# adaLN columns by transposes, and a routing whose shift stands inside the product sets

## The chip, the cores and the metric

One core of a Trainium2 chip runs the whole program. The metric is the device time of one execution in microseconds (us). TensorE multiplies, VectorE and ScalarE work elementwise, GpSimd does a few small powers, and the queue of SyncE (SP) issues the weight transfers. A single engine's instructions run in the order written into its queue.

## The reference

Two layers over 256 rows of 1024 features: a gated linear attention, then a gated recurrence, each followed by 16 experts of which two work on a row. All arithmetic is in 32-bit floats. In each layer six vectors of 1024 come from the conditioning vector (shift, scale and gate, for the mixer and for the experts): this is called adaLN here.

```python
def rmsnorm(x, g):
    inv = lax.rsqrt(jnp.mean(x * x, axis=-1, keepdims=True) + EPS)
    return (x * inv) * g

def modulate(h, shift, scale):
    return h * (1 + scale[:, None]) + shift[:, None]

def gla_mixer(h, w_in, w_gate_up, b_gate, norm_g, w_out):
    proj = h @ w_in
    q, k, v, g, a_lr = jnp.split(proj, [512, 1024, 2048, 3072], axis=-1)
    log_a = jax.nn.log_sigmoid(a_lr @ w_gate_up + b_gate) / 16
    # chunks of 64 rows: cumulative sums of log_a, decayed k, a state per chunk
    # S_n = diag(G_n) S_{n-1} + k_dec^T v,  o = q S_n,  o = rmsnorm(o) * silu(g)
    return o @ w_out

def lru_mixer(h, w_in, ...):
    gate_br, xb = jnp.split(h @ w_in, 2, axis=-1)
    # causal convolution of 4 taps, two gates by 4 blocks of 256, a scan over time
    return (hs * jax.nn.gelu(gate_br)) @ w_out

def grouped_moe(h, router_w, router_bias, w_gate, w_up, w_down):
    scores = jax.nn.sigmoid(h @ router_w)
    # the group with the best two biased scores, the best two experts in it
    for e in range(16):
        he = jax.nn.silu(h @ w_gate[e]) * (h @ w_up[e])
        out = out + combine[:, e:e + 1] * (he @ w_down[e])
    return out

def reference(x, c, ...):
    cond = jax.nn.silu(c)
    for i in range(2):
        sh1, sc1, g1, sh2, sc2, g2 = jnp.split(cond @ ada_w[i] + ada_b[i], 6, axis=-1)
        h = modulate(rmsnorm(x, norm_mix_g[i]), sh1, sc1)
        mix = gla_mixer(h, ...) if i == 0 else lru_mixer(h, ...)
        x = x + g1[:, None] * mix
        h = modulate(rmsnorm(x, norm_ffn_g[i]), sh2, sc2)
        x = x + g2[:, None] * grouped_moe(h, router_w, ...)
    return rmsnorm(x, final_norm_g)
```

## The kernel before, in words

**Weights.** Nearly all bytes are weights, 285 MB, and each is used once. They stream through a ring of 17 slots of 1 MB (`Stream`, `SLOTS`). `plan` writes the order out by hand; `stream.get` takes the next slot and lets the queue run ahead. The queue issues in that order, and a transfer whose slot is still in use holds all behind it. The same ring also lends slots to large intermediate tiles (`big`).

**adaLN.** Each of the six vectors per layer needs a product of 1024 by 1024, read as two halves of 512 columns, 2 MB each. `fill` does a half on VectorE: eight multiply-adds (L335, L333) leave 128 partial sums per column in `acc`, at a lower priority than the rest. `fill_now` does it on TensorE in four quadrants (L354) and copies the result (L356), which leaves each column's four sums in rows 0, 32, 64 and 96. What is left is put in `owed`, and `settle` finishes it: for a gate vector, wanted along the free dimension, a product with ones (L365) and a copy; for shifts and scales, wanted as one column of a partition each, a product with ones or with the selector `quad` (L368), a masked product with the identity (L370), a reduction (L371), and small sums with the tables (L373 to L376). `bent` applies a scale and a shift to a transposed tile of features (L438 on ScalarE, L440 on VectorE).

**First layer.** `gla` normalizes x, transposes it (L448) and needs the mixer's columns in two halves. `bend(0)` computes the first column set, settles it and bends four of the eight feature tiles; then three token projections take their first halves (L565), `bend(1)` does the second set, the low-rank products follow (L575), and then the second halves, with the gate's cumulative sums (L595, L598) between the second and the third projection.

**Out product and routing.** `out_route` multiplies by the out weights in four parts (L488), adds to x (L490, L491) and routes in between, with TensorE's order fixed as written. Behind the third settle stand `router` (the router's weights times the scale, L803; the shift's share of the scores, a tiny product, L806, spread over the rows, L808), then the parts of the second row block, with transposes and `logits` (L817) between products. `choose` picks experts on VectorE, `route_count` counts rows (L855, L858), `gather_tile` collects rows (L908), and `route_order` sorts the experts by load. Only then are the routed weights' addresses known (L937), and their transfers can be issued (L263).

**Experts.** `moe` runs seven units: the first with two experts that are always loaded, the others in the order found. A unit is two up products (L1016), an activation (L1133, L1134), transposes (L1145), a down product (L1027) and a scatter into x (L1046, L1047). Unit 0 also spreads the row weights and settles what is owed; units 3 and 4 transpose h for `overflow`, a branch for rows that found no room, which the data of this run doesn't enter. The last unit runs in column parts (L1038).

## Time and profile before

| | |
|---|---|
| time, median of 3 runs | 796.24 us (795.29 to 800.42) |
| profiled execution, its own time | 796.28 us |
| its span | 794.5 us |
| TensorE busy (its share) | 729.8 us (92%) |
| VectorE busy | 356.0 us (45%) |
| ScalarE busy | 137.5 us (17%) |
| HBM read | 284.54 MB, 359 GB/s over the span |

Busy shares are means over stages with different limits, and TensorE's ends are modelled, so 92% doesn't say that TensorE sets the time. The rows below are read by stage: who waits, for whom, and whether the DMA engines are full at that time. PE is TensorE (PEld its weight loads), DVE VectorE, ACT ScalarE, POOL GpSimd, SPq the queue of SyncE.

### The profile page before, as it was taken

What the parts mean: (1) busy time and instruction counts of PE and PEld (TensorE: products, weight loads), DVE (VectorE), ACT (ScalarE), POOL (GpSimd) and SP (SyncE); (2) the same over time, 40 slices, a digit from 0 to 9 for tenths busy, and PEclk for the clock granted to TensorE, in tenths of its full rate; (3) what the DMA queues carried; (4) which work ended last, traced back from release to release, by engine and by line L of the source; (5) the groups of instructions that cost most, each with busy time, mean ns of one, the idle gap of its engine ahead of it and who ended that gap; (6) DMA issues with size and microseconds to landing.
All of it is one profiled execution on the core that took longest, in us unless ns stands there. A gap on an engine that the chain in (4) does not pass through costs nothing. (4 is left out here: it accounts for less than half of the span.)

```text
span 794.5 us, 9656 instructions
## 1 busy us (share of the span) xinstructions
PE 729.8 (92%) x3591; PEld 357.0 (45%) x3591; DVE 356.0 (45%) x809; ACT 137.5 (17%) x271; POOL 27.1 (3%) x69
## 2 busy tenths in 40 slices
PE   4889999988999999998978999978899999999984
PEld 3333664445353353353215888635553353353322
DVE  3225876687462142231114389985632233222114
ACT  4104213021120011010003147121120011010002
POOL 4000001000000000000000005000000000000000
PEclk9899999999999999999998999989799999999999
DMA  9999969678879999999999999982599999999994
GB/s 297 386 387 387 385 239 318 202 282 361 342 317 423 419 421 422 420 419 413 420 370 378 375 363 332 403 326 106 230 408 397 420 420 419 421 422 407 421 379 156
DMA packets 80445, 286.27 MB, mean 360 GB/s; under 512 B 5991, under 2 KB 16280, under 8 KB 57866
## 3 DMA queue, kind: packets, MB, share of 16 engines
q1 hardware_dynamic: 78752, 284.71, 92.2%
q10 hardware_dynamic: 1258, 0.66, 0.3%
q8 instruction: 30, 0.49, 0.3%
q0 software_dynamic: 384, 0.23, 0.1%
q14 instruction: 21, 0.17, 0.1%
HBM read 284.54 MB, written 1.05 MB: 359 GB/s over the span
## 5 line engine op out<-in xcount | busy, mean ns | idle before, releaser
L1016 PE MATMUL ps<-w 128*32 128x512 f32 (+1 forms) x1280 | 201.8, 594 | 4.8 <-DMA w<-in_moe_w_up_dram 2.9
L1016 PEld LDWEIGHTS ps<-w 128*32 128x32 f32 (+1 forms) x1280 | 62.5, 121 | 137.7 <-issue 120.2
L1027 PE MATMUL ps<-w,s 128*32 128x512 f32 (+1 forms) x512 | 85.0, 594 | 2.8 <-ACT s L1147 2.8
L1047 DVE TENSOR_TENSOR x<-x,ps 128x512 f32<-128x512 f32 (+1 forms) x60 | 39.1, 652 | 56.7 <-PE ps L1046 56.6
L488 PE MATMUL ps<-w 128*128 128x512 f32 x128 | 61.6, 627 | 0.0
L1046 PE MATMUL ps<-mid,s 128*128 128x512 f32 (+1 forms) x120 | 55.1, 581 | 2.9 <-DVE mid L1155 2.6
L1134 DVE TENSOR_TENSOR s<-s,ps 128x512 f32<-128x512 f32 x14 | 9.6, 686 | 105.6 <-PE ps L1016 105.6
L733 PE MATMUL ps<-hT,w 128*128 128x256 f32 x256 | 56.7, 384 | 0.0
L333 DVE SCALAR_TENSOR_TENSOR acc<-w,cond,acc 128x512 f32<-128x512 f32 x70 | 54.0, 801 | 0.7
L733 PEld LDWEIGHTS ps<-hT,w 128*128 128x128 f32 x256 | 49.4, 194 | 6.9
L1027 PEld LDWEIGHTS ps<-w,s 128*32 128x32 f32 (+1 forms) x512 | 25.6, 123 | 58.3 <-issue 51.8
L565 PE MATMUL ps<-w,hT 128*128 128x512 f32 x96 | 46.3, 638 | 3.5 <-issue 3.5
L1166 DVE TENSOR_TENSOR mid<-ps,gate 128x512 f32<-128x512 f32 x24 | 16.6, 692 | 63.2 <-PE ps L1027 63.2
L890 PE MATMUL ps<-onehot,h 128*128 128x256 f32 x192 | 42.4, 379 | 0.0
L333 DVE SCALAR_TENSOR_TENSOR gate<-w,cond,gate 128x512 f32<-128x512 f32 x56 | 40.9, 747 | 0.9
L890 PEld LDWEIGHTS ps<-onehot,h 128*128 128x128 f32 x192 | 36.5, 190 | 7.5 <-issue 2.4
L1133 ACT ACTIVATE s<-ps 128x512 f32<-128x512 f32 x14 | 8.4, 599 | 164.4 <-PE ps L1016 164.4
L488 PEld LDWEIGHTS ps<-w 128*128 128x128 f32 x128 | 24.4, 201 | 25.5 <-issue 24.0
L1046 PEld LDWEIGHTS ps<-mid,s 128*128 128x128 f32 x120 | 20.5, 190 | 30.8 <-issue 20.8
L565 PEld LDWEIGHTS ps<-w,hT 128*128 128x128 f32 x96 | 19.2, 204 | 28.4 <-issue 27.9
L1147 ACT COPY s<-ps 128x512 f32<-128x512 f32 x14 | 8.2, 586 | 136.1 <-PE ps L1145 136.1
L370 DVE TENSOR_TENSOR s<-ps,ident 128x512 f32<-128x512 f32 x16 | 10.6, 680 | 43.3 <-PE ps L368 43.3
(267 smaller groups left out, 688.8 us busy)
## 6 DMA issues: line engine op xcount, KB each, us to landing
w<-in_moe_w_gate_dram SPq DMA_DIRECT2D x64, 1024.0 KB, 10.0
w<-in_moe_w_up_dram SPq DMA_DIRECT2D x64, 1024.0 KB, 13.1
w<-in_moe_w_down_dram SPq DMA_DIRECT2D x56, 1024.0 KB, 15.8
w<-in_ada_w_dram SPq DMA_DIRECT2D x48, 1024.0 KB, 11.6
w<-in_gla_w_in_dram SPq DMA_DIRECT2D x12, 1024.0 KB, 14.5
w<-in_moe_w_down_dram SPq DMA_DIRECT2D x16, 512.0 KB, 10.0
w<-in_lru_w_in_dram SPq DMA_DIRECT2D x8, 1024.0 KB, 12.4
w<-in_gla_w_out_dram SPq DMA_DIRECT2D x4, 1024.0 KB, 4.8
```

Source lines behind the costliest of these rows:

```text
L333: V.scalar_tensor_tensor(acc, w, cond[:, k:k + 1], acc, op0=OP.mult, op1=OP.add)
L370: V.tensor_tensor(own, ps.rearrange("p (q j) -> p q j", j=4), ident[:, :, None].to_broadcast([P, P, 4]), op=OP.mult)
L488: T.matmul(ps, yT[:, k, m * P:(m + 1) * P], w[k // 2][:, k % 2, sl], start=k == 0, stop=k == 7)
L565: T.matmul(pst[i][m], hT[:, 4 * b + j, m * P:(m + 1) * P], w[:, j], start=b == 0 and j == 0, stop=b == 1 and j == 3)
L733: T.matmul(ps[:, 0:S], w[k // 4][:, k % 4, ct * P:(ct + 1) * P], hT[:, k, :], start=k == 0, stop=k == 7)
L890: T.matmul(ps[j // 2][:, j % 2 * 2 * P:(j % 2 + 1) * 2 * P], hv[:, b, j, :], oh, start=m == 0 and j % 2 == 0, stop=m == 1 and j % 2 == 1, ...
L1016: T.matmul(ps[p0:p0 + n], xg[:, k, t0 + p0:t0 + p0 + n], w[i][:, j, :], start=k == 0, stop=k == 7)
L1027: T.matmul(ps[hf][p0:p0 + n], aT[:, k, p0:p0 + n], w[i][:, j, hf * 512:(hf + 1) * 512], start=k == 0, stop=k == 3)
L1046: T.matmul(ps, wt[:, m * P:(m + 1) * P], y[:, sl], start=True, stop=True)
L1047: V.tensor_add(x[:, m, sl], x[:, m, sl], ps)
L1134: V.tensor_mul(act, act, pu)
L1166: V.tensor_mul(y[:, sl], py[hf], g2[:, sl])
```

## The change

`settle` makes columns by four transposes of the accumulated rows and one reduction that reads their result, over all 128 entries or, after `fill_now`, over the four that count; the product with ones, the masked product and `quad` go. The second column set of `gla` is computed after two projections instead of three, and is settled and bent inside the third, between its two row blocks; the state's key projection closes ahead of the cumulative sums. In `out_route` the settle of the shift and the router's share of it go into the third part's products, the scores are split from `logits`, the row count of the second block follows four gather products, and in layer two the gate's sums and the final gain's rows are made here instead of in the experts. The overflow's transposes go into its branch. The first small tables of the gate are issued on ScalarE's queue instead of GpSimd's.

```diff
     for q in range(4):
-        G.dma_start(gtab[32 * q:32 * q + 16], I["gla_w_gate_up"][0])
-    G.dma_start(gtab[16:17], I["gla_b_gate"])
+        A.dma_start(gtab[32 * q:32 * q + 16], I["gla_w_gate_up"][0])
+    A.dma_start(gtab[16:17], I["gla_b_gate"])
     V.tensor_scalar(e16, pid, 16.0, None, op0=OP.is_equal)
...
         for _ in range(min(n, len(owed))):
-            acc, dst, r, gain, sel = owed.pop(0)
+            acc, dst, r, gain, four = owed.pop(0)
             ps = bank()
             if dst is None:
-                T.matmul(ps, sel, acc, start=True, stop=True)
+                T.matmul(ps, ones, acc, start=True, stop=True)
                 A.copy(acc, ps)
                 continue
-            T.matmul(ps, sel, acc, start=True, stop=True)
-            own = s2("own").rearrange("p (q j) -> p q j", j=4)
-            V.tensor_tensor(own, ps.rearrange("p (q j) -> p q j", j=4), ident[:, :, None].to_broadcast([P, P, 4]), op=OP.mult)
-            V.tensor_reduce(dst, own.rearrange("p q j -> p j q"), axis=AX.X, op=OP.add)
+            for j in range(4):
+                T.transpose(ps[:, j * P:(j + 1) * P], acc.rearrange("r (p j) -> r j p", j=4)[:, j, :], ident)
+            rows_of = ps.rearrange("p (j q r) -> p j q r", j=4, q=4)[:, :, :, 0] if four else ps.rearrange("p (j q) -> p j q", j=4)
+            V.tensor_reduce(dst, rows_of, axis=AX.X, op=OP.add)
             if gain is None:
...
         return h, hT
-    def out_route(l, yT, gate, gs, rest=None):
+    def out_route(l, yT, gate, gs, rest=None, last=None):
...
             if rest:
                 rest()
-            settle(2)
             router(R, gs)
-            part(1, 0, {3: first, 6: lambda: logits(R, hT, 0, stats_of[0])})
+            part(1, 0, {2: lambda: settle(2), 4: first, 6: lambda: router_shift(R, gs[1], 0), 7: lambda: logits(R, hT, 0)})
+            router_shift(R, gs[1], 1)
+            scores(R, 0, stats_of[0])
             choose(R, 0)
             fill(2)
-            part(1, 1, {3: lambda: turn_h(x, hT, 1, halves=[0]), 5: lambda: logits(R, hT, 1, None, halves=[0]),
+            part(1, 1, {3: lambda: turn_h(x, hT, 1, halves=[0]), 5: lambda: logits(R, hT, 1, halves=[0]),
                         7: lambda: route_count(R, 0)})
...
                 accs = mid("acc")
                 fill_now(accs[:, 0:512])
+            else:
+                settle(1)
             turn_h(x, hT, 1, halves=[1])
             xg, oh = gather_begin(R)
             gather_tile(R, h, oh, 0, 0, [0])
-            logits(R, hT, 1, r, halves=[1])
+            logits(R, hT, 1, halves=[1])
+            scores(R, 1, r)
             scaled(h, 1, r)
             gather_tile(R, h, oh, 0, 0, [1, 2, 3])
             choose(R, 1)
+            gather_tile(R, h, oh, 0, 1)
             route_count(R, 1)
-            gather_tile(R, h, oh, 0, 1)
             if late:
                 fill_now(accs[:, 512:1024])
+            else:
+                settle(1)
+            if last:
+                last()
             gather_end(l, R, h, xg, gs)
...
         def bend(b):
-            fill_now()
-            fill_now()
             settle()
...
         pst = [[None] * NM for _ in range(3)]
-        def half_proj(i, b):
-            w = stream.get("i").rearrange("p (j n) -> p j n", j=4)
+        def half_proj(i, b, between=None, w=None):
+            w = (stream.get("i") if w is None else w).rearrange("p (j n) -> p j n", j=4)
             for m in range(NM):
+                if m and between:
+                    between()
                 if b == 0:
...
                              stop=b == 1 and j == 3)
+        fill_now()
+        fill_now()
         bend(0)
-        for i in range(3):
-            half_proj(i, 0)
-        bend(1)
+        half_proj(0, 0)
+        half_proj(1, 0)
+        with tc.manual_schedule(engines={T.engine}):
+            w2 = stream.get("i")
+            fill_now()
+            fill_now()
+            half_proj(2, 0, lambda: bend(1), w2)
         ps = bank()
...
         for m in range(NM):
             A.copy(v[:, m, 512:1024], pst[1][m])
+        half_proj(2, 1)
         psg = bank()
...
         A.activation(gam, psg[:, 0:16], AF.Exp, scale=1.0 / 16.0)
         kd = h.rearrange("p m (c n) -> p (m c) n", c=2)
-        half_proj(2, 1)
         for m in range(NM):
...
     def router(R, gs):
-        g, s = gs
-        w, b, bb = rt("rw", 8, NE), sm.tile([1, NE], F32, name="r_b", bufs=1), rt("bb", NE)
-        V.tensor_tensor(w, rw, g[:, :, None].to_broadcast([P, 8, NE]), op=OP.mult)
-        at = R["ps"][:, 3 * NE:4 * NE]
-        for k in range(8):
-            T.matmul(at[0:1], s[:, k:k + 1], rw[:, k, :], start=k == 0, stop=k == 7)
-        V.tensor_copy(b, at[0:1])
-        T.matmul(at, ones[0:1, :], b, start=True, stop=True)
-        V.tensor_copy(bb, at)
-        R.update(rw=w, bb=bb, lg=[bank() for _ in range(NM)])
-    def logits(R, hT, m, r, halves=(0, 1)):
+        w = rt("rw", 8, NE)
+        V.tensor_tensor(w, rw, gs[0][:, :, None].to_broadcast([P, 8, NE]), op=OP.mult)
+        R.update(rw=w, lg=[bank() for _ in range(NM)])
+    def router_shift(R, s, at):
+        ps = R["ps"][:, 3 * NE:4 * NE]
+        if at == 0:
+            R["b"] = sm.tile([1, NE], F32, name="r_b", bufs=1)
+            for k in range(8):
+                T.matmul(ps[0:1], s[:, k:k + 1], rw[:, k, :], start=k == 0, stop=k == 7)
+            V.tensor_copy(R["b"], ps[0:1])
+        else:
+            R["bb"] = rt("bb", NE)
+            T.matmul(ps, ones[0:1, :], R["b"], start=True, stop=True)
+            V.tensor_copy(R["bb"], ps)
+    def logits(R, hT, m, halves=(0, 1)):
...
             for k in range(4 * b, 4 * b + 4):
                 T.matmul(ps, hT[:, k, m * P:(m + 1) * P], R["rw"][:, k, :], start=k == 0, stop=k == 7)
-        if 1 in halves:
-            z = rt("z", NE)
-            V.scalar_tensor_tensor(z, ps, r, R["bb"], op0=OP.mult, op1=OP.add)
-            A.activation(R["sc"][:, m], z, AF.Sigmoid)
+    def scores(R, m, r):
+        z = rt("z", NE)
+        V.scalar_tensor_tensor(z, R["lg"][m][:, 0:NE], r, R["bb"], op0=OP.mult, op1=OP.add)
+        A.activation(R["sc"][:, m], z, AF.Sigmoid)
...
         R["sr"] = sr.rearrange("p (q t) -> p q t", q=4)
-    def moe(l, h, hT, R, gs, g2, more=None, done=None):
+    def moe(l, h, hT, R, gs, g2, done=None):
         def prepare(w, su):
...
                 flag = nc.values_load(R["flag"][0:1, 0:1], min_val=0, max_val=1)
             with tc.If(flag > 0):
+                bent_before = mark["bent"]
+                for m in range(NM):
+                    turn_h(h, hT, m, gs)
+                mark["bent"] = bent_before
                 co = sm.tile([P, NM, NE], F32, name="o_co", bufs=1)
...
             if u:
                 settle()
-            if u == 1 and more:
-                more()
-            if u in (3, 4):
-                turn_h(h, hT, u - 3, gs)
             pu = up_proj(unit, xg, t0)
...
         fg.append(wk.tile([P, D], F32, name="gate", bufs=2))
         for hf in range(2):
-            V.tensor_copy(fg[0][:, hf * 512:(hf + 1) * 512], bcast_row(FINAL + hf))
+            ps = bank()
+            T.matmul(ps, ident[:, FINAL + hf:FINAL + hf + 1].to_broadcast([P, P]), tab, start=True, stop=True)
+            A.copy(fg[0][:, hf * 512:(hf + 1) * 512], ps)
+    h, hT, R = out_route(1, yT, g1, gf, last=final_gain)
...
```

## Rows read from the trace of the kernel before

**Rows 1.** The page's forty slices: busy share of the DMA engines, in tenths.
```profile
DMA  9999969678879999999999999982599999999994
```

**Rows 2.** Windows: us, five engines busy (instructions), granted clock, DMA share, GB/s.
```profile
198.00:202.00 4.00, 4.00 (x27) 1.74 (x27) 1.33 (x6) 0.59 (x1) 0.00 (x0) 0.75 0.24 59
...
230.00:240.00 10.00, 9.27 (x52) 3.59 (x54) 5.25 (x13) 1.60 (x3) 0.00 (x0) 1.00 0.56 213
...
590.00:600.00 10.00, 9.32 (x55) 3.05 (x58) 2.64 (x6) 0.98 (x2) 0.00 (x0) 1.00 0.91 355
```

**Rows 3.** Timeline of layer two's order: start us, us, engine, line, operation, tiles, count.
```profile
563.06 2.69 SPq L263 DMA_DIRECT2D w<-in_moe_w_gate_dram  x4
```

**Rows 4.** Timeline of the first bend; in brackets idle before, and what ended it.
```profile
21.88 0.59 ACT L356 COPY acc<-ps 128x512 f32<-128x512 f32 x1 [1.13 <-PE ps L354]
...
22.90 0.69 DVE L370 TENSOR_TENSOR s<-ps,ident 128x512 f32<-128x512 f32 x1 [4.80 <-PE ps L368]
...
23.63 1.05 DVE L371 TENSOR_REDUCE gs<-s 128x4 f32<-128x512 f32 x1
...
26.27 0.15 DVE L376 TENSOR_TENSOR gs<-gs,tabT 128x4 f32<-128x4 f32 x1
...
27.17 1.19 PE L565 MATMUL ps<-w,hT 128*128 128x512 f32 x1 [3.45 <-issue]
```

**Rows 5.** Timeline of the second bend, TensorE alone.
```profile
50.71 3.64 PE L354 MATMUL ps<-w,cond 128*32 128x512 f32 x32
...
59.63 1.33 PE L575 MATMUL ps<-hT,mid 128*32 128x256 f32 x6 [2.80 <-DVE hT L440]
...
63.72 6.28 PE L565 MATMUL ps<-w,hT 128*128 128x512 f32 x14
```

**Rows 6.** Timeline of the first layer's routing, TensorE alone.
```profile
162.91 1.88 PE L368 MATMUL ps<-acc,one 128*128 128x512 f32 x4
...
168.94 4.54 PE L488 MATMUL ps<-w 128*128 128x512 f32 x6
...
173.31 0.63 PE L448 MATMUL ps<-ident,x 128*128 128x128 f32 x4
```

**Rows 7.** Timeline of layer two's expert order, VectorE: the nearest small reduction.
```profile
561.65 0.35 DVE L935 TENSOR_REDUCE r_ordf<-s 128x14 f32<-128x196 f32 x1
```

**Rows 8.** Windows, columns as in rows 2: granted clock around transposes and waits.
```profile
14.00:17.00 3.00, 3.00 (x16) 2.97 (x14) 1.08 (x2) 2.20 (x4) 0.00 (x0) 1.00 1.07 301
...
26.00:32.60 6.60, 5.43 (x7) 2.36 (x8) 1.29 (x5) 1.09 (x2) 0.00 (x0) 0.50 1.05 386
...
429.00:435.50 6.50, 5.78 (x22) 5.08 (x23) 3.90 (x7) 3.90 (x5) 0.00 (x0) 0.50 1.05 384
```

**Rows 9.** Waits of TensorE: line, waited for, us in total, times, longest us.
```profile
PE ps L806 <- DVE sh L373: 7.4, 3, 3.0
...
PE ps L858 <- DVE r_ohs L849: 3.2, 2, 1.8
...
PE ps L448 <- DVE x L491: 3.0, 3, 1.6
...
PE ps L598 <- DVE mid L588: 1.1, 1, 1.1
...
PE ps L448 <- DVE h L431: 0.9, 1, 0.9
```

**Rows 10.** The page's groups: busy us, mean ns of one, idle before.
```profile
L333 DVE SCALAR_TENSOR_TENSOR acc<-w,cond,acc 128x512 f32<-128x512 f32 x70 | 54.0, 801 | 0.7
```

**Rows 11.** Timeline of layer two's routing, TensorE alone.
```profile
522.86 1.88 PE L368 MATMUL ps<-acc,one 128*128 128x512 f32 x4
...
531.13 3.65 PE L488 MATMUL ps<-w 128*128 128x512 f32 x4
```

**Rows 12.** Timeline of the start: ScalarE's queue, and a weight load's wait.
```profile
5.02 1.29 ACTq L188 DMA_DIRECT2D mid<-in_gla_w_in_dram  x2
...
20.35 0.12 PEld L354 LDWEIGHTS ps<-w,cond 128*32 128x32 f32 x4 [0.31 <-DMA w<-in_ada_w_dram]
```

More of the change, by code (lines that the diff above doesn't have):

```diff
@@ L136, in trunk @@
     V.memset(after[64:128, 0:64], 0.0)
-    quad = cst.tile([P, 1], F32, name="quad")
-    V.memset(quad, 0.0)
-    for j in range(4):
-        V.memset(quad[32 * j:32 * j + 1], 1.0)
     half = cst.tile([P, 16], F32, name="half")
@@ L295, in trunk @@
     plan(1, "i2 i3 a20 r i0 a21 a40 i1 a41 a30 a31 o a50 a51 u0 u1 u2 u3 u4 u5 u6")
-    def bcast_row(r, n=512):
-        ps = bank()
-        T.matmul(ps[:, 0:n], ident[:, r:r + 1].to_broadcast([P, P]), tab[:, 0:n], start=True, stop=True)
-        d = s2("gain")
-        A.copy(d[:, 0:n], ps[:, 0:n])
-        return d[:, 0:n]
     tabT = cst.tile([P, 4, 64], F32, name="tabT")
@@ L338, in fill @@
             if wide:
-                owed.append((acc, None, None, None, ones))
+                owed.append((acc, None, None, None, False))
             else:
-                owed.append((acc, dst[:, 4 * hf:4 * hf + 4], r, gain + hf if gain is not None else None, ones))
+                owed.append((acc, dst[:, 4 * hf:4 * hf + 4], r, gain + hf if gain is not None else None, False))
     def fill_now(acc=None):
@@ L356, in fill_now @@
         A.copy(acc, ps)
-        owed.append((acc, dst[:, 4 * hf:4 * hf + 4], r, gain + hf if gain is not None else None, quad.to_broadcast([P, P])))
+        owed.append((acc, dst[:, 4 * hf:4 * hf + 4], r, gain + hf if gain is not None else None, True))
     def settle(n=99):
         for _ in range(min(n, len(owed))):
-            acc, dst, r, gain, sel = owed.pop(0)
+            acc, dst, r, gain, four = owed.pop(0)
             ps = bank()
             if dst is None:
-                T.matmul(ps, sel, acc, start=True, stop=True)
+                T.matmul(ps, ones, acc, start=True, stop=True)
                 A.copy(acc, ps)
                 continue
-            T.matmul(ps, sel, acc, start=True, stop=True)
-            own = s2("own").rearrange("p (q j) -> p q j", j=4)
-            V.tensor_tensor(own, ps.rearrange("p (q j) -> p q j", j=4), ident[:, :, None].to_broadcast([P, P, 4]), op=OP.mult)
-            V.tensor_reduce(dst, own.rearrange("p q j -> p j q"), axis=AX.X, op=OP.add)
+            for j in range(4):
+                T.transpose(ps[:, j * P:(j + 1) * P], acc.rearrange("r (p j) -> r j p", j=4)[:, j, :], ident)
+            rows_of = ps.rearrange("p (j q r) -> p j q r", j=4, q=4)[:, :, :, 0] if four else ps.rearrange("p (j q) -> p j q", j=4)
+            V.tensor_reduce(dst, rows_of, axis=AX.X, op=OP.add)
             if gain is None:
@@ L1062, in load @@
                     def load(name, n, j, q):
-                        t = wk.tile([P, NM, D], F32, name="h").rearrange("p m n -> p (m n)")
+                        t = h.rearrange("p m n -> p (m n)")
                         nc.sync.dma_start(t, I[name][l][ds(e, 1), q * n:(q + 1) * n, :]
@@ L1185, in trunk @@
     yT = lru(h, hT, *k0)
-    h, hT, R = out_route(1, yT, g1, gf)
     fg = []
@@ L1200, in done @@
             V.tensor_mul(o[m][:, sl], x[:, m, sl], fg[0][:, sl])
-    moe(1, h, hT, R, gf, g2, final_gain, done)
+    moe(1, h, hT, R, gf, g2, done)
     r = rsqrt2(ss)
```

## The prediction

> **What bounds the kernel now.** I read the forty slices first. The DMA row [rows 1] is full in three stretches: the first 100 us, the first expert layer from about 240 us, and the second from about 570 us. Between them, from 100 to 240 us and from 530 to 570 us, it has holes. An expert layer is therefore paid in bytes. Its end is fixed by when its routed weights may start, and TensorE work inside it is free as long as the ring of 17 slots does not run dry. In the holes the weights wait for TensorE and VectorE.
>
> The windows, read next, show the price. At 198 to 202 us, around the first order, DMA is 0.24 busy (3.0 us lost); at 230 to 240 us 0.56 (4.4 us lost), and at 590 to 600 us 0.91 (0.9 us lost) [rows 2]. The last two are the ring standing full until the first unit's down products release slots. The first routed load of layer two goes out at 563.06 us [rows 3], and from there it is bytes to the end. So the sum is made of what shortens the way to the two orders, and what shortens the two stalls behind them.
>
> From 8 to 100 us DMA is also full, which would speak for a byte bound there. Against it: in this stretch TensorE waits for VectorE with weights already landed [rows 4, 5], and from 100 to 200 us the row's digits are 6 9 6 7 8, so up to 1.3 slices of 19.9 us, or 26 us, are empty [rows 1]. Earlier slot releases can be used there.
>
> **The change part by part.** The sum is made against the profiled execution, 796.28 us (its span 794.50 and 1.8 around it), which is the median of the runs, 796.24, within 0.01%. A difference under 1% is what a measurement here cannot tell from none.
>
> *A, first bend.* Today: the second column set's copy ends at 22.47 us, then come a product with ones, a masked product on VectorE of 0.69 and a reduction of 1.05 for each column, and small operations of about 0.15; the first projection starts at 27.17, after 3.45 us of idle and 0.75 after the last small operation on the gain ends [rows 4]. New: four transposes, 0.63 us as in [rows 6], and a reduction over 16 elements. No row has this reduction; the nearest is 196 elements in 0.35 us [rows 7], and the 512-element one of 1.05 is the upper end. I take 0.3, because 16 elements lie beyond the small one. Then the same 0.75 for the shift's sum and the first bend: 22.47 + 0.63 + 0.3 + 0.75 = 24.15. Gain **3.0 us** (2.2 with the upper end).
> After today's wait the granted clock is 0.50, the lower level of 1.2 GHz, from 26.0 to 32.6 us [rows 8], so 3.3 us are lost. Before the 16 transposes at 14 to 17 us TensorE idled 0.9 us [rows 9], and the clock stood at 1.00 [rows 8]. I take the **3.3**, from zero to that.
>
> *B, second bend.* Between 50.71 and 63.72 us TensorE does two column sets, the settle, the low-rank products and two projection instructions, with 2.80 us of waiting and a half-speed stretch behind it [rows 5]: 13.0 us. New: the two column sets (3.64), eight transposes (1.26), the low-rank products (16 at the rate of 6 in 1.33 are 3.5 at half speed, half that at full: 1.8) and two projection instructions (0.45 each, 14 in 6.28): 7.6. The chain on VectorE lies under the four token products of the second half, 8 instructions of 0.45 = 3.6 us, and needs about what A's needs, two reductions and twice the 0.75, 2.1. It fits; if fills cut in, the rest comes back as a wait, at most today's 2.80. Gain **5.4**.
>
> *C, state projection ahead of the cumulative sums.* It fills the wait of 1.1 us for VectorE [rows 9]. **1.1**.
>
> *D, E, F, first routing.* Settling two ones-columns costs 1.88 us and will cost 1.26 [rows 6]. The row stands six times: at 145, 163, twice near 221, at 506 and 523 us. The one at 145 gives **D 0.6**. In the routing, 162.91 to 168.94 are 6.03 us [rows 6], of which 3.0 are the wait for the shift columns [rows 9]. The rest, 6.03 - 3.0 - 1.88 = 1.15, are the shift's tiny products and copies; they stay. New: 1.26 + 1.15 = 2.4, gain 3.6. The half-clock stretch behind it (169.4 to 172.6, the second of the pattern in [rows 8]) gives 1.6 more: 5.2. Behind the order the settle of four columns loses 2 x 0.62 = 1.2, so the down products come 6.4 earlier. Can DMA follow? It has 3.0 + 4.4 = 7.4 us of holes here. The brake is VectorE: the fills of 8 operations a column, 0.8 us each [rows 10], release the slots of the first unit's last tiles; they get about 1.1 us a column from the dropped masked product and shorter reduction (0.35/196 x 512 = 0.9 at most for 512 elements, against 0.69 + 1.05). **E and F 6.4**, between 3.0 and 7.4.
>
> *G, H, I, layer two.* Settle at 506 us: **G 0.6**. Routing: 522.86 to 531.13 are 8.27 us [rows 11]; 4.4 are the two shift waits (7.4 in all less the longest, 3.0, which is the first routing's [rows 9]). New 2.4, so 5.9, and 1.7 for the stretch at half clock to 534.5 (the pattern of [rows 8]; four products take 3.65 us there [rows 11]). VectorE is full in this stretch, and every critical operation can stand behind one fill of 0.8; I take off 1.0. **H 6.6**. The gate's two sums (0.94 each) and the final gain's two products move from the experts to the waits for the last rows and the second choice (the longest of each kind 1.6 and 1.8 us [rows 9]; no term of their own). They gain **I 0.9**, the stall at 590 us. Moving the count behind four gather products costs at most 0.6 us if the clock is low there; I take 0.
>
> *Edits at nothing.* The five first-table loads: two such issues hold ScalarE 1.29 us [rows 12], so its squares start up to 3.2 us later, while GpSimd is free earlier. But the first column products wait for their weights at 20.35 us [rows 12], and what comes before has that long. From -0.5 to +1.5. The overflow's sixteen transposes and their bends leave units 3 and 4 of both layers, where DMA is full and TensorE not the bound [rows 1]: 0, both ends under 0.5. The branch isn't entered. If the ring were empty there, the cover would be gone, and they would give 1 us a unit.
>
> Sum: 3.0 + 3.3 + 5.4 + 1.1 + 0.6 + 6.4 + 0.6 + 6.6 + 0.9 = 27.9, so 796.3 - 27.9 = **768.4 us**.
>
> **A rule against it.** The 16 transposes at 14 us ran at a granted 1.00, but those at 430 us began and ended at 0.50, and the clock rose only when products followed [rows 8]. The Trainium skill, "TensorE: Matmul & The Clock Gate", Part 4: PE-mode transpose, states that transposes do not count as busy in the same way, so a settle made of them would look idle to the clock. By it the sum would be the second rival's 783, without it 768.
>
> **The rivals.**
> 1. *Forecast*: 768. For it: the waits named are TensorE's longest after the start [rows 9], and DMA has room.
> 2. *The clock falls at every settle of the new kind*, because they add to the quiet time. Then A's 3.3 and the clock gains in B (about 1.9), E (1.6) and H (1.7) go, and the settles at 145 and 506 us, dense today, would cost a stretch like A's each, 6.6: 768.4 + 15.1 = 783. Against it: the first row of [rows 8].
> 3. *VectorE takes the place of the wait.* The critical reductions and residual adds queue behind fills in its in-order queue, and the slots follow the fills. Then E and F fall to 3.0 and H to 2: 768.4 + 3.4 + 4.6 = 776. For it: VectorE is the engine that the two shift waits end on [rows 9].
> 4. *The first layer is bytes already.* Then only G, H and I remain: 796.3 - 8.1 = 788. Against it: the holes [rows 1, 2].
> 5. *Slower*: the fixed order on VectorE puts whole low-priority fills ahead of the new reductions. A pair of columns is 16 fills of 0.8 = 12.8 us [rows 10]. In the second bend and both routings, TensorE would stand that long: 3 x 12.8 = 38, less what is gained anyway, 28: 806. It decides from the third place on; with two it is 794. Against it: today the fills stand singly between critical operations, and TensorE's waits for the shift columns are 3.0 us at most [rows 9].
>
> **How the numbers follow.** Forecast 0.50, clock 0.18, VectorE 0.22, bytes 0.06, slower 0.04. The predicted time is the first, 768. The range reaches from all upper ends (E and F 7.4, no loss in H, start -0.5: 2.5 less; and some 4 us if denser work also lifts the half-clock stretches after 197 and 555 us, of the pattern in [rows 8]) to the clock's 783: 762 to 783. Left out are bytes and slower, 0.10, and about as much at the edges. Faster by over 1% means under 788.3: 0.91; within 1% 0.05; slower by over 1% 0.04.
>
> **What would show it.** Right: the first projection near 24 us with the clock at 1.00; no wait of the low-rank products; no wait for the shift columns; the first routed load of layer two some 27 us earlier than 563; DMA over 0.9 in the slices that hold today's 198 to 202 and 230 to 240. Wrong: a granted 0.50 behind settles, TensorE waiting on residual adds or on the first choice's counts, or the DMA row full from 100 us on with the orders still late.

## The result and the profile after

The changed kernel takes **761.97 us** (median of 4 runs, 760.81 to 762.6) against 796.11 us (4 runs, 795.29 to 800.42): a ratio of **0.956**, 95% interval 0.952 to 0.960. That is 34.1 us less, where 768 was predicted with a range from 762 to 783; the time lies just under the low end. Its profiled span is 760.7 us at a mean granted clock of 0.985, against 794.5 us.

The page's slices come first: granted clock and DMA share.

```profile
PEclk9999999999999999999998999999999999998998
DMA  9999999779999999999999999991999999999994
```

Against [rows 1], the holes in the first third have shrunk to two slices of 7, and the second low stretch, 8 2 5 9, is 9 1 9 9. Next the first bend, with ScalarE's queue ahead of it (start us, us, engine, line, operation, tiles; in brackets idle time before, and its releaser):

```profile
6.44 3.70 ACTq L187 DMA_DIRECT2D mid<-in_gla_w_gate_up_dram  x4
...
11.02 0.63 ACT L381 ACTIVATE s<-x 128x512 f32<-128x512 f32 x1 [6.11 <-DMA mid<-in_gla_w_gate_up_dram]
...
23.40 1.53 PE L356 MATMUL ps<-ident,acc 128*128 128x128 f32 x8
...
24.19 0.17 DVE L359 TENSOR_REDUCE gs<-ps 128x4 f32<-128x16 f32 x1 [4.17 <-PE ps L356]
...
25.97 1.53 PE L561 MATMUL ps<-w,hT 128*128 128x512 f32 x3 [1.03 <-issue]
```

The wait of 3.45 us [rows 4] is 1.03, and the short reduction costs 0.17 us, so the settle itself did better than forecast. But the four table loads held ScalarE for 3.70 us, and everything up to the settle came later. TensorE's second bend, and its waits (line, waited for, us in total, times, longest):

```profile
46.98 1.12 PE L356 MATMUL ps<-ident,acc 128*128 128x128 f32 x8
...
51.46 1.07 PE L577 MATMUL ps<-hT,mid 128*32 128x256 f32 x16
52.46 7.13 PE L561 MATMUL ps<-w,hT 128*128 128x512 f32 x16
```

```profile
PE ps L1025 <- PEq L1062: 4.1, 1, 4.1
...
PE ps L436 <- DVE h L419: 3.1, 2, 1.7
...
PE ps L867 <- DVE r_ohs L858: 2.3, 2, 1.4
...
PE ps L436 <- DVE x L479: 0.7, 1, 0.7
```

No instruction in the second bend shows idle time before it, where [rows 5] had 2.80. The waits for the shift columns (7.4) and for the gate's cumulative sums (1.1) of [rows 9] are gone, those for the choices fell from 3.2 to 2.3, and those for the residual rows from 3.0 to 0.7. Of the waits for VectorE, the one that grew is that for normalised rows at the start (0.9 to 3.1, two waits). In the experts of layer two a wait of 4.1 us at the branch of `overflow` (L1062) is new. The time doesn't show it: the kernel with the overflow's transposes back in the units (below) has no such wait and takes as long.

The order of layer two now leaves at 530.75 us instead of 563.06 [rows 3], 32.3 us earlier:

```profile
530.75 2.11 SPq L258 DMA_DIRECT2D w<-in_moe_w_gate_dram  x3
```

The following table cuts the span at the same points in both timelines. The forecast's letters stand beside the stretches.

| Stretch | before, us | after, us | gained | forecast |
|---|---|---|---|---|
| to the first projection (A) | 27.17 | 25.97 | 1.2 | 3.0 |
| to the query products (A's clock, B, C) | 62.96 | 52.42 | 10.5 | 9.8 |
| to the out product of layer one (D) | 57.14 | 56.36 | 0.8 | 0.6 |
| to the LRU's products (E and F) | 286.04 | 275.85 | 10.2 | 6.4 |
| to the out product of layer two (G) | 74.43 | 73.78 | 0.7 | 0.6 |
| to the order of layer two (H) | 55.32 | 46.37 | 8.9 | 6.6 |
| to the end (I) | 231.44 | 229.95 | 1.5 | 0.9 |
| sum | 794.50 | 760.70 | 33.8 | 27.9 |

So no stretch lost time. E and F exceed their upper bound of 7.4, H exceeds its value by 2.3, and A falls short. A's 1.2 is also a lucky start: in seven more traces of kernels with this beginning, all from the experiments below, the first projection lies between 26.55 and 27.95 us, against 27.17 before. Windows over the stretch of E and F show how (us, TensorE busy and instructions, granted clock, DMA share, GB/s), first of before:

```profile
104.24:147.27 43.03, 43.03 (x150) 1.00 0.84 284
147.27:200.41 53.14, 46.77 (x198) 0.94 0.73 274
200.41:240.00 39.59, 38.86 (x184) 1.00 0.86 347
240.00:433.31 193.31, 181.69 (x1072) 0.98 1.02 411
```

and then of after, between the same events, with 219 us for 240:

```profile
92.50:134.75 42.25, 42.25 (x153) 1.00 0.99 369
134.75:181.69 46.94, 45.05 (x215) 1.00 0.82 312
181.69:219.00 37.31, 36.63 (x186) 1.00 0.95 384
219.00:410.60 191.60, 178.48 (x1045) 0.98 1.02 411
```

Length times what is missing to 1.00 gives DMA's empty time: 6.9 + 14.3 + 5.5 = 26.7 us before and 0.4 + 8.4 + 1.9 = 10.7 after. The bound of 7.4 had counted only the holes behind 198 us.

### The profile page after: what moved, and what is told of

Same layout as the page of the kernel before. It is cut to its first block, busy times and chain, and to the rows that moved or that the text cites. A ratio compares the mean times of both kernels' runs of the same rounds, so it can differ in the third digit from the quotient of the medians.

```text
span 760.7 us, 9585 instructions
## 1 busy us (share of the span) xinstructions
PE 706.8 (93%) x3591; PEld 348.2 (46%) x3591; DVE 330.0 (43%) x766; ACT 132.8 (17%) x259; POOL 24.6 (3%) x64
## 3 DMA queue, kind: packets, MB, share of 16 engines
HBM read 284.54 MB, written 1.05 MB: 375 GB/s over the span
## 5 line engine op out<-in xcount | busy, mean ns | idle before, releaser
L1025 PE MATMUL ps<-w 128*32 128x512 f32 (+1 forms) x1280 | 204.6, 598 | 10.3 <-DMA w<-in_moe_w_up_dram 4.8
L476 PE MATMUL ps<-w 128*128 128x512 f32 x128 | 59.3, 600 | 0.0
L561 PE MATMUL ps<-w,hT 128*128 128x512 f32 x96 | 42.3, 595 | 1.0 <-issue 1.0
L476 PEld LDWEIGHTS ps<-w 128*128 128x128 f32 x128 | 22.8, 191 | 20.7 <-issue 19.1
L532 PE MATMUL ps<-w,hT 128*128 128x512 f32 x64 | 28.0, 592 | 0.0
```

Source lines behind the costliest of these rows:

```text
L476: T.matmul(ps, yT[:, k, m * P:(m + 1) * P], w[k // 2][:, k % 2, sl], start=k == 0, stop=k == 7)
L532: T.matmul(ps, hT[:, k, m * P:(m + 1) * P], w[k // 4][:, k % 4, :], start=k == 0, stop=k == 7)
L561: T.matmul(pst[i][m], hT[:, 4 * b + j, m * P:(m + 1) * P], w[:, j], start=b == 0 and j == 0, stop=b == 1 and j == 3)
L1025: T.matmul(ps[p0:p0 + n], xg[:, k, t0 + p0:t0 + p0 + n], w[i][:, j, :], start=k == 0, stop=k == 7)
```

## Experiments

Two theories stood at the start. **Waits**: each part of the change shortens waits of TensorE on the path to an order, DMA has room to follow, and the clock falls less as TensorE stands less. **VectorE**: what counts is its lighter load (356.0 to 330.0 us busy), which releases the ring's slots earlier wherever it is saved. All edits start from the changed kernel, but for the one that says otherwise; times are medians, ratios are against the kernel before beside it.

### The parts of the change, taken back one at a time

**Tables back on GpSimd's queue.**

```
     for q in range(4):
-        A.dma_start(gtab[32 * q:32 * q + 16], I["gla_w_gate_up"][0])
-    A.dma_start(gtab[16:17], I["gla_b_gate"])
+        G.dma_start(gtab[32 * q:32 * q + 16], I["gla_w_gate_up"][0])
+    G.dma_start(gtab[16:17], I["gla_b_gate"])
```

> The changed kernel with the five first-table loads back on GpSimd's queue, all else as changed. Theory of waits (the gain is TensorE's waits and the half-clock stretches behind them): the five issues held ScalarE from 6.4 to 11.0 us and made the first column products end at 23.4 us instead of 21.8, so this kernel's first projection starts near 24.4 us and everything after it 1.2 to 1.6 us earlier: 760.5 us. Theory of VectorE (the gain is VectorE's lighter load, which releases ring slots earlier): nothing of VectorE's load changes, 762.0 us.

760.5 us, ratio 0.954 (0.950 to 0.958). The first projection starts at 23.91 us, 2.06 earlier than in the changed kernel, with the clock at 1.00, and this lead is kept to 134 us (out product 1.83 earlier). At the LRU's products it is 1.3. So the table loads cost 2 us at the start, or up to 4 by the later starts of the other traces, and the settle alone is worth 27.17 - 23.91 = 3.3 there. In the whole time the difference of 1.5 us is within the intervals.

**Old places in the routing**, with the new settle.

```
+            settle(2)
             router(R, gs)
-            part(1, 0, {2: lambda: settle(2), 4: first, 6: lambda: router_shift(R, gs[1], 0), 7: lambda: logits(R, hT, 0)})
+            router_shift(R, gs[1], 0)
             router_shift(R, gs[1], 1)
-            scores(R, 0, stats_of[0])
+            part(1, 0, {3: first, 6: lambda: (logits(R, hT, 0), scores(R, 0, stats_of[0]))})
```

> The changed kernel with the settle of the shift and the whole shift of the router ahead of the third part's products again, settle still by transposes. Theory of waits: in both routings TensorE stands for two reductions and sums, about 2 us, does 1.1 us of tiny products in the open, and the granted clock falls for some 3 us behind it, 1.6 us lost: 3 to 4.5 us a layer, 768 to 771 us, with the first routed load of layer two 6 to 9 us later than in the changed kernel. Theory of VectorE: its load is that of the changed kernel, 762 to 763 us.

769.93 us, ratio 0.965 (0.961 to 0.969). The first shift product on TensorE, then its waits for the shift columns:

```profile
154.64 0.55 PE L814 MATMUL ps<-rw,sh 128*1 128x16 f32 x16 [1.81 <-issue]
```

```profile
PE ps L814 <- DVE sh L361: 2.5, 2, 1.6
```

The shift waits are back, and the two routings took 3.5 and 4.7 us longer (out product to order). Its VectorE is as light as in the changed kernel, 330.2 us, yet it is 8 us slower: the theory of VectorE falls as it stands. What the lighter load adds beside the shorter waits is not separated; the overflow's transposes back in the units (below) raise the load by 7 us, to 336.9, at no cost.

**Old settle, new places.**

```
-            for j in range(4):
-                T.transpose(ps[:, j * P:(j + 1) * P], acc.rearrange("r (p j) -> r j p", j=4)[:, j, :], ident)
...
-            V.tensor_reduce(dst, rows_of, axis=AX.X, op=OP.add)
+            T.matmul(ps, quad.to_broadcast([P, P]) if four else ones, acc, start=True, stop=True)
+            own = s2("own").rearrange("p (q j) -> p q j", j=4)
+            V.tensor_tensor(own, ps.rearrange("p (q j) -> p q j", j=4), ident[:, :, None].to_broadcast([P, P, 4]), op=OP.mult)
+            V.tensor_reduce(dst, own.rearrange("p q j -> p j q"), axis=AX.X, op=OP.add)
```

> The changed kernel with settle by a product with ones or quadrants, a masked product and a long reduction as before; all places as changed. Theory of waits: the first bend loses 3.0 us and gets its half-clock stretch back (3.3), every pair costs TensorE 0.7 us more on six places, and in the routings the longer chain on VectorE is partly hidden: 762 plus 9 to 13 us, 771 to 775 us. Theory of VectorE: with 16 masked products and reductions back, some 20 us of its load, most of the gain goes: 780 us or more.

775.44 us, ratio 0.972 (0.968 to 0.976): 13.5 us lost: 3.8 at the first projection (29.76 us), 3.9 from there to the query products, 0.8 from those to the out product, 3.1 in the first routing, 2.4 from its order to the LRU, and 1.4 in the second routing, while the end was 1.4 shorter.

**Old order in the first mixer**, with the new settle: the second bend behind the three first halves, and the state projection behind the cumulative sums.

```
-        half_proj(0, 0)
-        half_proj(1, 0)
-        with tc.manual_schedule(engines={T.engine}):
-            w2 = stream.get("i")
-            fill_now()
-            fill_now()
-            half_proj(2, 0, lambda: bend(1), w2)
+        for i in range(3):
+            half_proj(i, 0)
+        fill_now()
+        fill_now()
+        bend(1)
...
-        half_proj(2, 1)
...
+        half_proj(2, 1)
```

> The changed kernel with the attention's old order: three half projections, then the second column set with its settle and bends in the open, and the state projection behind the cumulative sums. Theory of waits: the low-rank products wait about 2 us for the chain on VectorE, which may or may not bring the clock down (1.9), and the wait of 1.1 us for the cumulative sums returns: 765 to 767 us, seen already in the start of the query products. Theory of VectorE: its load is the same, 762 to 763 us.

766.14 us, ratio 0.961 (0.957 to 0.965). From the first projection to the query products it needs 55.72 us, 3.3 more, and the wait of C is back as in [rows 9]:

```profile
PE ps L598 <- DVE mid L588: 1.1, 1, 1.1
```

### What the first bend does to the clock

Here the first bend alone was given its old settle, and the gap that it leaves on TensorE was left open, filled with products, or filled with transposes (neither filling's output is used).

```
     def bend(b):
-        settle()
+        settle(first=b == 0)
+        if b == 0:
+            junk = bank()
+            for i in range(24):
+                T.transpose(junk[:, i % 4 * P:(i % 4 + 1) * P], strict, ident)
```

With `first` set, `settle` does the old product, masked product and reduction. In the first kernel the last four lines are missing; in the second four products of 512 columns stand in place of the 24 transposes.

> The changed kernel with the old settle (quadrant product, masked product, long reduction) in the first bend alone. Theory of waits: TensorE stands some 3 us again, and the granted clock falls to 0.50 for 6 to 7 us behind it; from the first projection to the query products it takes 52.4 + 3.3 = 55.7 us. Theory that the wait alone costs: the first projection is 2 to 3 us later and the 52.4 us behind it stay.

> As the kernel with the old settle in the first bend, with four idle products of 128 by 512 (result not used) in TensorE's queue where it would stand. If the clock falls because TensorE stands: the clock stays at 1.00, the first projection starts where it did without them or up to 0.5 us later, and from there to the query products it takes 52.4 us. If it falls because of what was done before (column products and settles), it still falls and takes 55.7.

> As the last, with 24 transposes of 128 by 128 (result not used) in the place of the four products, about the same length. By the rule that transposes do not count as busy, the clock falls as if TensorE stood: 55.7 us from the first projection to the query products. If transposes hold the clock as products do: 52.4.

768.49, 765.08 and 766.58 us, a single time each. The open gap, timeline and windows of TensorE:

```profile
30.62 9.93 PE L571 MATMUL ps<-w,hT 128*128 128x512 f32 x19 [3.46 <-issue]
...
28.00:32.00 4.00, 1.38 (x2) 0.79 1.05 388
32.00:36.00 4.00, 4.00 (x8) 0.78 1.05 384
```

and the gap filled with transposes:

```profile
27.30 2.78 PE L561 MATMUL ps<-ident,strict 128*128 128x128 f32 x24
31.00 9.25 PE L575 MATMUL ps<-w,hT 128*128 128x512 f32 x21 [0.92 <-issue]
...
28.00:32.00 4.00, 3.08 (x23) 1.00 1.05 386
32.00:36.00 4.00, 4.00 (x11) 1.00 1.05 385
```

From the first projection to the query products the three need 53.96, 52.41 and 52.42 us. So the clock fell to its lower level behind the open gap of 3.46 us, at a cost of 1.5 us here, and 24 transposes kept it up as four products did. The cost is not the same in every execution. In the kernel before, the 48 products of the three first halves took 23.54 us behind a gap of 3.45 (27.17 to 50.71 [rows 4, 5]). After the change 32 such products took 13.90, until the second column set began, which makes 20.85 for 48, so the gap had cost 2.7:

```profile
39.87 3.64 PE L341 MATMUL ps<-w,cond 128*32 128x512 f32 x32
```

**Tables on ScalarE's queue, but behind the normalisation.**

```
-    for q in range(4):
-        A.dma_start(gtab[32 * q:32 * q + 16], I["gla_w_gate_up"][0])
-    A.dma_start(gtab[16:17], I["gla_b_gate"])
...
         h, hT = norm()
+        for q in range(4):
+            A.dma_start(gtab[32 * q:32 * q + 16], I["gla_w_gate_up"][0])
+        A.dma_start(gtab[16:17], I["gla_b_gate"])
```

> The changed kernel with the five first-table loads on ScalarE's queue behind the first rows' normalization. Theory of waits: ScalarE's squares start near 7.8 us and GpSimd's queue is free for the powers, so the transposes of x are done by 16 us; the column products then wait for their weights and the first projection starts at 23.5 to 24.4 us, as with the tables on GpSimd's queue: 759 to 761 us. If the start is bound by bytes before that: no better than 762.

760.11 us, ratio 0.954 (0.953 to 0.956). The squares start at 7.87 us again and the first projection at 24.31, but the clock falls behind it:

```profile
22.53 0.75 PE L353 MATMUL ps<-ident,acc 128*128 128x128 f32 x4 [0.70 <-ACT acc L340]
24.31 7.94 PE L561 MATMUL ps<-w,hT 128*128 128x512 f32 x14 [1.03 <-issue]
...
24.00:26.00 2.00, 1.69 (x3) 0.82 1.05 386
26.00:28.00 2.00, 2.00 (x4) 0.50 1.05 388
28.00:30.00 2.00, 2.00 (x5) 0.82 1.05 384
```

The query products come 54.12 us after it, not 52.42: the 1.7 us gained are given back at once. The same idle of 1.03 us left the clock at 1.00 in the changed kernel; here a wait of 0.70 stands ahead of it.

### One part alone, and the unit work

The first is the kernel before with nothing but the new settle.

```
-            T.matmul(ps, sel, acc, start=True, stop=True)
-            own = s2("own").rearrange("p (q j) -> p q j", j=4)
-            V.tensor_tensor(own, ps.rearrange("p (q j) -> p q j", j=4), ident[:, :, None].to_broadcast([P, P, 4]), op=OP.mult)
-            V.tensor_reduce(dst, own.rearrange("p q j -> p j q"), axis=AX.X, op=OP.add)
+            for j in range(4):
+                T.transpose(ps[:, j * P:(j + 1) * P], acc.rearrange("r (p j) -> r j p", j=4)[:, j, :], ident)
...
+            V.tensor_reduce(dst, rows_of, axis=AX.X, op=OP.add)
```

> One part alone: the kernel before, with only the settle of a column accumulator changed to four transposes and a short reduction; every order of work stays as it was, and the first tables stay on GpSimd's queue. Theory of waits (each part of the change shortens waits of its own, and the parts add up): the changed kernel with the old settle was 13.5 us slower than the changed one, so this kernel should be about 13 to 15 us faster than the kernel before, 782 to 785; the first projection near 24 us, the wait of the low-rank products of the second bend still there but shorter than 2.8, the two longest shift waits down to about 1.5 to 2 us from 3.0 and 4.4. Theory of VectorE (what counts is the lighter load, some 26 us less of busy time, wherever it is): most of the gain comes with the settle alone, 765 to 772. Third theory (an order that leaves a wait open loses the gain, because the product still stands behind the shift): 788 to 793.

775.7 us, ratio 0.974 (0.971 to 0.978): 19.8 us faster than before, more than the parts' additivity allowed and less than VectorE's theory wanted. The shift wait remains, shorter:

```profile
PE ps L807 <- DVE sh L374: 4.4, 3, 1.9
```

Settle alone gives 19.8 us; the rest of the change with the old settle gives about 22 (775.44 against 797.72 in its own comparison); both together give 34. The parts overlap by some 8 us, because both shorten the same waits: 3.4 of it lie between the first projection and the query products, and 2.5 in the second routing. My expectation that they add up was wrong.

**All unit work back**: the overflow's transposes in units 3 and 4 of both layers, and the gate's two sums and the final gain's two products in the experts of layer two; both edits stand with the runs below that make them singly.

> The changed kernel, with the work that had left the expert units put back: the overflow's sixteen transposes run in units 3 and 4 of both layers, the gate's two sums and the final gain's two products in the experts of layer two. Theory of waits: the first worth 0 to 0.5, the second 0.9, so 762.5 to 763.5, and the lost time stands between the order of layer two and the end (231 instead of about 229.5 us). Rival (TensorE has become the bound in the experts, 93% busy as it is after the change): every moved instruction counts, about 1 us a unit for four units and 3.1 for the sums and products, 767 to 769. Rival (bytes alone): 762.0, no difference.

767.61 us, ratio 0.964 (0.960 to 0.967), against 762.25 us for the changed kernel beside it. That is the time of the rival with TensorE as the bound.

**The changed kernel once more.**

> The changed kernel itself once more, beside the other three on the same chip: 762 within 0.3%, so that differences of 1 to 2 us can be read. The first projection, which lay at 25.97, 26.55 and 27.95 us in three kernels with the same beginning, shows how far the start varies from one execution to the next.

762.25 us, ratio 0.957 (0.954 to 0.960), as before; its first projection lay at 26.72 us.

Five microseconds for what the forecast had at 0.9. The two moves were then put back separately.

```
-                for m in range(NM):
-                    turn_h(h, hT, m, gs)
...
+            if u in (3, 4):
+                turn_h(h, hT, u - 3, gs)
```

> The changed kernel, with only the overflow's sixteen transposes and their bends back in units 3 and 4 of both layers. Theory of the clock (what cost 5.4 us is the missing work in the waits of the second routing): 762.3 to 762.8, the clock at 1.00 around the second order, 0.7 us from that order to the first up product. Rival (TensorE is the bound inside the units): 764 to 766.

761.76 us, ratio 0.957 (0.955 to 0.959): the overflow's transposes cost nothing in the units, as forecast.

```
-            else:
-                settle(1)
...
-            else:
-                settle(1)
-            if last:
-                last()
...
+            if u == 1 and more:
+                more()
```

> The changed kernel, with only the gate's two sums and the final gain's two products back in the experts of layer two. Theory of the clock: nearly all of the 5.4 us, 766.5 to 767.5; a granted 0.50 before the second order, 2.5 us from the order to the first up product, and a wait of 2 us or more for the second choice. Rival (the units' own time): 763, as the step I of the forecast had it, with the clock at 1.00 around the order.

765.92 us, ratio 0.963 (0.961 to 0.965), 4.2 us more than the kernel just above: most of the five are these four products. In its second routing, timeline and windows:

```profile
520.32 1.10 PE L436 MATMUL ps<-ident,x 128*128 128x128 f32 x4 [1.60 <-DVE x L479]
...
522.20 1.89 PE L819 MATMUL ps<-r_rw,hT 128*128 128x16 f32 x8 [0.36 <-DVE hT L438]
...
530.09 3.40 PE L911 MATMUL ps<-onehot,h 128*128 128x128 f32 x16 [2.48 <-DVE onehot L886]
...
520.00:528.00 8.00, 6.94 (x32) 0.57 0.01 2
528.00:531.40 3.40, 1.31 (x8) 0.87 0.00 0
531.40:536.00 4.60, 4.60 (x22) 0.72 0.77 258
```

and in the changed kernel's second run:

```profile
521.72 1.07 PE L825 MATMUL ps<-r_rw,hT 128*128 128x16 f32 x8 [0.52 <-DVE hT L438]
...
520.00:526.00 6.00, 3.88 (x30) 1.00 0.00 0
526.00:530.20 4.20, 4.20 (x21) 1.00 0.00 0
530.20:535.00 4.80, 4.80 (x27) 1.00 0.75 265
```

Without the two sums and the gain's products TensorE waits 1.60 us instead of 0.74 for the last rows and 2.48 for the one-hots; the clock falls to the lower level, the same logits take 1.89 us instead of 1.07, and the first up product comes 2.5 us later (533.42 against 530.90), though the four products, 1.02, 1.10 and 1.88 us in that second run, are gone from the way to it. Behind it another 1.6 are lost in the experts. The products were worth more as filling of a wait than as work taken from a unit, and the rival's 767 to 769 came about mostly another way than it said.

**Count ahead of the gather again**, in both routings.

```
             choose(R, 1)
-            gather_tile(R, h, oh, 0, 1)
             route_count(R, 1)
+            gather_tile(R, h, oh, 0, 1)
```

> The changed kernel, with the count of the second row tile ahead of the four gather products of the first again, as before the change. If this order is what lifted the low clock behind the first order (2.43 us from the order to the first up product before, 0.53 after): 2 us later at the first up product, 763.5 to 764. If the denser work ahead of it lifted the clock: the stretch stays at 1.00, the order goes out up to 0.6 us earlier, 761.5 to 762.

767.58 us, ratio 0.964 (0.961 to 0.968): 5.3 us lost, more than either theory had. Around its second order, TensorE's timeline and windows:

```profile
529.20 0.61 PE L867 MATMUL ps<-r_ohs,strict 128*128 128x16 f32 x2 [2.28 <-DVE r_ohs L858]
...
529.00:534.00 5.00, 4.80 (x15) 0.50 0.00 0
534.00:538.50 4.50, 4.50 (x22) 0.86 0.77 260
```

The gather products had covered 0.9 us of the wait for the choice (1.38 in the kernel beside it). With the full 2.28 the clock falls; from the order to the first up product it is 4.05 us instead of 0.72 in layer two, and 2.46 instead of 0.53 in layer one.

## Why the prediction was too careful

**Mechanism right, sizes wrong.** Faster by over 1%, through shorter waits on the way to the two orders and DMA holes that let the weights follow: the table and the windows bear this out, and the settle, the places and the order, taken back one at a time, lost time in the stretches that the forecast had named for them. The clock's part was larger than forecast. In the kernel before it stood at 0.50 in six stretches that the change removed, near 26, 60, 169, 197, 528 and 555 us, and TensorE was busy 28.2 us in them. At twice the clock that work takes 14 us less, an estimate; in the profile after, none of the six is left.

**The step that failed is E and F: "6.4, between 3.0 and 7.4".** It measured 10.2. Cut at the order of layer one (200.41 and 181.69 us), the way to it gave 6.2, where 5.2 was forecast, and the way from it to the LRU 4.0, where 1.2 was. Two things were missing. First, the upper end counted the empty DMA time behind 198 us only [rows 2]; the 21 us of empty time between 104 and 200 us, which the first part of the prediction had itself seen in [rows 1], could be used too, and was: 26.7 us of it fell to 10.7. Second, "Moving the count behind four gather products costs at most 0.6 us ... I take 0" had the sign wrong. Where that count stands decides whether the clock is at 1.00 or lower behind an order: it gave 1.9 us at the first up product of layer one (2.43 to 0.53), as putting it back showed, and 5.3 us in all. The forecast knew the low stretches behind 197 and 555 us, but kept them out of the sum. TensorE was busy 3.4 and 8.2 us in them, so they were worth some 5.8 us, an estimate as above, near the 6.2 by which the sum fell short (27.9 against 34.1).

**H, 6.6, measured 8.9.** The 1.0 taken off for fills on VectorE ahead of critical operations was not lost: the second routing shows waits of 0.74, 0.52 and 1.38 us and none for the shift. The rest I put down to the clock; no run separates it. Around the order of layer two (563.06 and 530.75 us), windows of TensorE of the kernel before:

```profile
558.00:563.00 5.00, 4.14 (x17) 0.50 0.01 3
563.00:566.00 3.00, 3.00 (x17) 0.63 0.66 199
```

and of after:

```profile
526.00:530.70 4.70, 4.31 (x20) 1.00 0.00 0
530.70:533.70 3.00, 3.00 (x20) 1.00 0.60 180
```

The forecast had taken out the earlier half-speed stretch, to 534.5 us, and left this one in. The gate's sums "gain I 0.9" as work; put back, they cost 2.5 us up to the first up product and 1.6 in the experts. The "4 us if denser work also lifts the half-clock stretches" stood in the range and not in the sum. Put into it, the sum would have been about 764.

**A, 3.0, measured 1.2.** The settle gave 3.3; the tables at "-0.5 to +1.5" cost 2.1, and up to 4.0 in the other traces, so the first projection did not come near 24 us. The delay of the squares came as forecast (11.02 against 7.75 us, 3.3 where up to 3.2 was assumed), but the cover did not exist: "what comes before has that long" rested on a wait of 0.31 us for weights in the middle of the column products [rows 12], and these started at 19.23 us, 1.9 later than with the tables on GpSimd's queue (17.30).

**A's clock, B and C**, 9.8, measured 10.5: right in sum, by errors that cancel in part. A's clock, 3.3 in the forecast, cost the kernel before 2.7: the 6.6 us at half clock in [rows 8] hold only 5.43 of work, so half of them is too much. B gave 6.6, not 5.4: its pieces took 6.4 us instead of 7.6 (eight transposes 0.95, the low-rank products 1.00). **D and G** were right within 0.2. **Overflow at nothing** was right.

**The rivals.** The clock falling at every new settle did not occur: the clock stood at 1.00 behind all of them in the changed kernel, and 24 transposes held it as well as products did. The rule drawn from the Trainium skill, "TensorE: Matmul & The Clock Gate", Part 4: PE-mode transpose, that transposes do not count as busy in the same way, is not borne out by this case, as far as one execution of each filling shows. For the stretch at 430 us in [rows 8], on which the forecast rested it, the trace of before shows another candidate, a wait of 2.80 us right ahead of the 16 transposes, which no run took out:

```profile
429.73 3.79 PE L470 MATMUL ps<-ident,h 128*128 128x128 f32 x16 [2.80 <-DVE h L431]
```

VectorE in the wait's place would have left E and F at 3.0 and H at 2; they gave 10.2 and 8.9. Bytes in layer one would have left nothing ahead of G; the stretches there gave 22.7 us. Whole fills ahead of the short reductions did not show: no wait of TensorE for the new columns is left in the second bend or in the routings.

**A better version?** With the tables on GpSimd's queue the ratio is 0.954, and behind the normalisation 0.954, against 0.956 and 0.957 for the change as it is. The intervals overlap; that these are faster is likely from the start alone, but not shown. Open also stays why 1.03 us of idle ahead of the first projection left the clock alone in one kernel and not in another.

## What to carry to other kernels

When a wait is shortened, ask what the clock does behind it: a short product moved into a wait can be worth the half-speed stretch that it prevents besides its own time (here 2.5 of the 4 us that four products gave lay ahead of the first up product, and a swap of two lines was worth 5.3). When bounding how far DMA can follow an earlier order, count all empty time from the point where TensorE gets ahead, not only the holes behind the order. Parts that shorten the same wait don't add up: here 20 and 22 us gave 34. And one trace is not enough for the start: with the same beginning, the first projection lay anywhere between 25.97 and 27.95 us.

## What was not expected of the hardware

- The four table loads of 16 partitions held ScalarE's queue for 3.70 us at the start; two of the same loads, sent at 6.71 us with the squares behind them, took 1.12, and each of the two that followed later 0.32.
- A reduction over 16 elements a partition, read from PSUM, takes 0.17 us (128x4 out); over 512 elements it takes 0.685 (mean of ten), where the one of [rows 4], which read the masked product, took 1.05.
- Transposes of 128x128 fp32 alone kept the granted clock at 1.00 through a gap of 3.7 us of which they filled 2.78, in one execution.
